# Nine weight buffers, each with its own order of words: interleaving the two parts, the two k tiles and the columns

## The chip, the cores and the metric

One core of one Trainium2 chip runs the whole kernel in one launch. The metric is the device time of that launch in microseconds (us), the median over the runs. Durations of single instructions below are in nanoseconds (ns) where they say so.

## The reference

A two-layer encoder trunk on 256 tokens of width 2048, in float32. Layer 0 mixes with neighbourhood attention and sliding-window attention, layer 1 with differential attention; both layers then have cross-attention to 256 memory tokens and an MLP of width 8192 with a squared ReLU. Around every part stands an RMS norm. Cut to what matters here:

```python
def squared_relu_mlp(h, w_up, w_down):          # w_up (2048, 8192), w_down (8192, 2048)
    u = jax.nn.relu(h @ w_up)
    return (u * u) @ w_down

for layer in range(2):
    proj = rms_norm(h, mix_pre_g[layer]) @ w_in   # (2048, 4608) even, (2048, 6144) odd
    y = attention(proj) @ w_out                   # (2048, 2048)
    h = h + rms_norm(y, mix_post_g[layer])
    c = memory_cross_attention(rms_norm(h, mem_pre_g[layer]), mem_n, wq, wk, wv, wo)
    h = h + rms_norm(c, mem_post_g[layer])
    f = squared_relu_mlp(rms_norm(h, mlp_pre_g[layer]), w_up[layer], w_down[layer])
    h = h + rms_norm(f, mlp_post_g[layer])
```

## The kernel before

Every product is done in three matmuls. Both operands are split into a high part, rounded to the type fp32r, and a low part, the rest; high times high, high times low and low times high are added in PSUM (mm3, line 255; the list of pairs is PAIRS). An fp32r matmul takes a stationary operand of 128 x 128, which a weight load (LDWEIGHTS, shown as engine PEld) brings in, and streams a moving operand of up to 512 columns past it.

The weights come from memory once. Weights.load (line 177) makes one weight tile: a DMA on the queue of SP brings 256 rows by 512 columns as two k tiles of 128 rows into a buffer "raw" (three of them), ScalarE writes the high part (line 188, or 193 with the norm's gain) and VectorE the low part, raw minus high (line 189, or 194). The tile is called w and has on each partition 2 parts x 2 k tiles x 512 columns of four bytes, 8 KiB. Tiles rotate through NW = 9 buffers of the pool wp, the nine "homes"; a few (11) go to tiles of other names that are free at the time (tags v, qT, kT, lt). A home is filled again when its last matmul is done; matmuls ask for tiles AHEAD = 4 tiles before they need them.

There are three uses of a weight tile:

- in_block / in_step (line 263): projections. x, transposed and split, is the stationary operand, the weights are the moving operand: w[:, b, kk, :], 512 columns. A tile serves 2 token tiles x 2 k tiles x 3 = 12 matmuls. In the profile this is `mm<-w,xT` of line 257.
- out_block (line 289): output projections and the MLP's down product. Again the weights move, 12 matmuls a tile: `mm<-w,lt` of line 257.
- up (line 686, groups 1 to 15 of each layer's 16): the MLP's up product. Here the weights are stationary: for each 128 columns of one k tile, the high part is loaded and both parts of x stream past it as 512 columns (line 718), then the low part, and the high part of x streams past as 256 columns (line 719). A tile serves 8 such pairs. Group 0 of each layer goes through in_block.

The order of TensorE's instructions is written out by hand (a manual schedule with a clock of its own, the class Line); the other engines follow by semaphores. A pool "shift" of X_SHIFT = 24 words stands between the long-lived tiles (h, y, xT) and wp, so that all homes begin 96 bytes after where they would begin.

Of the kernel before, what the change touches and what calls it, by code (L numbers as in the profile page):

```python
# [12 lines left out]
F32R = mybir.dt.float32r  # L13
# [17 lines left out]
NPB = 2  # L31
X_SHIFT = 24
NG = 16
D_TR, D_EV, D_ROPE = 8, 3, 8
SW_GAP, SW_T, SW_M = 4, 8, 7
NA_GAP, NA_T, NA_M = 5, 14, 9
# [35 lines left out]
def trunk(  # L72
# [8 lines left out]
    keep = ctx.enter_context(tc.tile_pool(name="keep", bufs=1))  # L81
    shift = ctx.enter_context(tc.tile_pool(name="shift", bufs=1))
    shift.tile([P, X_SHIFT], F32, name="shift")
    wp = ctx.enter_context(tc.tile_pool(name="wp", bufs=NW))
    rawp = ctx.enter_context(tc.tile_pool(name="rawp", bufs=3))
    gp = ctx.enter_context(tc.tile_pool(name="gp", bufs=1))
    sb = ctx.enter_context(tc.tile_pool(name="sb", bufs=1))
# [67 lines left out]
    class Weights:  # L155
        def __init__(self):
            self.specs, self.tiles, self.n, self.wait, self.open = [], {}, 0, [], set()
            self.goal, self.live = -1, 0

        def plan_in(self, src, n0, g, spare=(), gate=None):  # L160

# [7 lines left out]
        def plan_out(self, src, k0):  # L169
# [4 lines left out]
                    self.specs.append((src, k0 + 2 * kp, n * 512, None, None, None))  # L174
            return a

        def load(self, j):
            src, k0, n0, tag, _, g = self.specs[j]
            raw = rawp.tile([P, 2, 512], F32, tag="raw", name="raw")
            nc.sync.dma_start(  # L180
                raw, src[k0 * P : (k0 + 2) * P, n0 : n0 + 512].rearrange("(k p) n -> p k n", p=P)
            )
            if tag is None:
                w = wp.tile([P, 2, 2, 512], F32R, tag="w", name="w")
            else:
                w = sb.tile([P, 2, 2, 512], F32R, tag=tag, bufs=1, name="w")
            if g is None:
                A.copy(w[:, 0], raw)  # L188
                V.tensor_tensor(w[:, 1], raw, w[:, 0].bitcast(F32), ALU.subtract)  # L189
            else:  # L190
                for kk in range(2):
                    gk = gains[:, g * KT + k0 + kk : g * KT + k0 + kk + 1]
                    A.activation(w[:, 0, kk], raw[:, kk], AF.Copy, scale=gk)  # L193
                    V.scalar_tensor_tensor(  # L194
                        w[:, 1, kk], raw[:, kk], gk, w[:, 0, kk].bitcast(F32), ALU.mult, ALU.subtract
                    )
            self.tiles[j] = w
# [57 lines left out]
    def mm3(pt, lhs, rhs, first, last):  # L255
        for i, (a, b) in enumerate(PAIRS):
            PE.matmul(pt, lhs(a), rhs(b), start=first and i == 0, stop=last and i == 2)  # L257

    def xT_lhs(kt, t):
        return lambda a: xT[:, kt, a, t, :]  # L260

    def in_step(pt, u, kp, t):
        w = W.get(u + kp)
        line.until(lambda: I.has_x(t, kp // 2, W.specs[u + kp][5] >= G_MN))
        for kk in range(2):
            kt = 2 * kp + kk
            mm3(pt, xT_lhs(kt, t), lambda b: w[:, b, kk, :], kt == 0, kt == KT - 1)
            if kk == 1 and t == NT - 1:
                W.done(u + kp)
            line.tick()  # L270
# [19 lines left out]
    def out_block(u, lt, first, done=None, stagger=False):  # L290
        def chunk(t, n):
            pt = mm_ps()
            for kt in range(4):
                w = W.get(u + 2 * n + kt // 2)
                mm3(
                    pt, lambda a: lt[:, a, kt, t * P : (t + 1) * P], lambda b: w[:, b, kt % 2, :],
                    kt == 0, kt == 3,
                )
                if kt % 2 == 1 and t == NT - 1:
                    W.done(u + 2 * n + kt // 2)  # L300
                line.tick()
            ysl = y[:, t, n * 512 : (n + 1) * 512]
            if done is not None:
                if first:
                    done(t, n, pt)
                else:
                    V.tensor_tensor(ysl, pt, ysl, ALU.add)  # L307
                    done(t, n, ysl)
            elif first:
                A.copy(ysl, pt)  # L310
            else:
                V.tensor_tensor(ysl, pt, ysl, ALU.add)  # L312

        order = [(t, n) for t in range(NT) for n in range(4)]
        for t, n in order if stagger else sorted(order, key=lambda x: x[1]):
            chunk(t, n)
# [337 lines left out]
    def mem_and_mlp(l, R, kT, nxt):  # L654
        qT = qT_tile()

        def between(t):
            for n in range(4):
                mem_x(t, n)

        in_block(U["mq", l], evac_T(qT, R, q=True, ev=D_EVM), lag=L_MQ, between=between)
        v = v_tile()
        hd = Heads(qT, kT, lambda i: i, v, lambda i: i, tags=("pT", "pT", "qT", "kT"), lag=(ME_GAP, ME_T, ME_M)).start(M_AT, mix=False)
        in_block(U["mv", l], evac_V(v, RSM), lag=L_MV)
        for i in range(4):
            line.until(lambda: hd.pT[i] is not None)
            hd.mix(i)
        lv = Leave(gain(mem_post_g[l : l + 1]), G_MLP + l)
        hd.finish()
        W.free(("up", l))  # L670
        out_block(U["mo", l], hd.lt, True, lv, stagger=True)
        R = lv.next

        def split_u(ut, j, pts):

            s = sb.tile([P, 512], F32, tag="p", bufs=NPB, name="s")
            for i, pt in enumerate(pts):
                e = sb.tile([P, S], F32, tag="ue", bufs=2, name="ue")
                A.copy(e, pt[:, S:])  # L679
                V.tensor_tensor(s[:, i * S : (i + 1) * S], pt[:, :S], e, ALU.add)  # L680
            A.activation(s, s, AF.Relu)
            A.activation(s, s, AF.Square)
            d = [ut[:, a, j : j + 2, :].rearrange("p k c -> p (k c)") for a in range(2)]
            split_to(d[0], d[1], s)

        def up(g):
            ut = lt_tile(("lt", "qT")[g % 2])
            if g == 0:
                left = [0, 1]

                def ev(t, pt):
                    q = sb.tile([P, 512], F32, tag="q", bufs=2, name="u")
                    A.activation(q, pt, AF.Relu)

                    def turn():
                        tp = tr_ps()
                        for i in range(4):
                            PE.transpose(tp[:, i * P : (i + 1) * P], q[:, i * P : (i + 1) * P], ident)
                        s = sb.tile([P, 512], F32, tag="p", bufs=NPB, name="s")
                        A.activation(s, tp, AF.Square)  # L700
                        sv = s.rearrange("p (k c) -> p k c", c=P)
                        split_to(ut[:, 0, :, t * P : (t + 1) * P], ut[:, 1, :, t * P : (t + 1) * P], sv)

                    line.later(D_EVU, turn)

                in_block(U["up", l, 0], ev, lag=L_UP)
                return ut
            pts = [at_ps() for _ in range(3)] + [mm_ps()]
            for kp in range(8):
                w = W.get(U["up", l, g] + kp)  # L710
                for t in range(NT):
                    line.until(lambda: I.has_x(t, kp // 2, False))
                for nt in range(4):
                    for kk in range(2):
                        kt = 2 * kp + kk
                        wn = [w[:, a, kk, nt * P : (nt + 1) * P] for a in range(2)]
                        both = xT[:, kt].rearrange("p a t c -> p (a t c)")
                        PE.matmul(pts[nt], wn[0], both, start=kt == 0, stop=False)  # L718
                        PE.matmul(pts[nt][:, :S], wn[1], both[:, :S], start=False, stop=kt == KT - 1)  # L719
                    if nt == 3:  # L720
                        W.done(U["up", l, g] + kp)
                    line.tick()
            for b in range(2):
                split_u(ut, 2 * b, pts[2 * b : 2 * b + 2])
            return ut

        uts = {0: up(0)}
        lv = None
        for g in range(NG):
            if g + 1 < NG:  # L730
                uts[g + 1] = up(g + 1)
            last = g == NG - 1
            if last and l == 0:
                W.free("odd")
            if last:
                eps = []
                for r in R:
                    q = sm.tile([P, 1], F32, tag="r2", name="r2")
                    V.tensor_tensor(q, r, r, ALU.mult)
                    V.reciprocal(q, q)  # L740
                    V.tensor_scalar(q, q, q, NEPS, ALU.mult, ALU.mult)
                    eps.append(q)
                lv = Leave(gain(mlp_post_g[l : l + 1]), nxt, eps)
            out_block(U["dn", l, g], uts.pop(g), g == 0, lv, stagger=last)
        return lv.next
# [233 lines left out]
```

## Time and profile before

| | us |
|---|---|
| median of 2 runs | 2386.59 |
| lowest, highest | 2384.79, 2388.38 |
| the profiled execution, time | 2386.64 |
| the profiled execution, span from the first to the last instruction | 2384.8 |
| mean granted TensorE clock in the span | 0.997 of full |

The profile shows one execution, whose time is 0.05 us from the median. PE is TensorE's matmuls, PEld its weight loads, DVE is VectorE, ACT is ScalarE, L257 is line 257. Matmuls overlap: the duration of one is from its start to the end of its last column through the array, so what a stream of them costs is read from start to start and not from the mean duration.

### The profile page before, as it was taken

How to read it: one execution, taken by the hardware profiler on the slowest of the kernel's cores; microseconds unless marked ns; L12 is line 12 of the kernel's file. 1: busy time of each engine (PE TensorE's matmuls, PEld its weight loads, DVE VectorE, ACT ScalarE, POOL GpSimd, SP SyncE). 2: the span in 40 equal slices, each digit the busy share in tenths (PEclk: the TensorE clock that was granted, in tenths of full speed). 3: DMA queues.
4: the chain of work that ended last, by engine and by line, in shares of the span. 5: the costliest groups of instructions: out<-in, count | busy, mean ns of one | idle time of the engine just before them, and what ended most of it. 6: DMA issues, size and time to landing. Idle time of an engine off the chain costs nothing.

```text
span 2384.8 us, 32033 instructions
## 1 busy us (share of the span) xinstructions
PE 2359.4 (99%) x11687; PEld 1985.5 (83%) x11687; DVE 1610.2 (68%) x2545; ACT 1374.4 (58%) x2280; POOL 28.0 (1%) x46
## 2 busy tenths in 40 slices
PE   8999999999999999999999999999999999999998
PEld 7788888888888888888888888887888888888887
DVE  5766678856656656656876667787666666666666
ACT  6756567755545545545666555676655555555543
POOL 0000000000000000000000000000000000000000
PEclk9999999999999999999999999999999999999999
DMA  7657655565665665665565555655665565665663
GB/s 240 217 181 236 187 192 194 183 203 179 194 194 181 194 195 182 195 193 186 184 194 170 172 189 169 200 186 177 198 194 187 186 196 184 191 196 180 194 194 114
DMA packets 238278, 451.88 MB, mean 189 GB/s; under 512 B 21288, under 2 KB 22184, under 8 KB 237352
## 3 DMA queue, kind: packets, MB, share of 16 engines
q1 hardware_dynamic: 237832, 449.32, 59.3%
q8 instruction: 91, 1.49, 0.3%
q14 instruction: 67, 0.55, 0.1%
q10 hardware_dynamic: 288, 0.52, 0.1%
HBM read 445.59 MB, written 5.15 MB: 189 GB/s over the span
## 4 chain that ended last, share of the span: by engine, by line
PE 91%; DMA 3%; DVE 3%; ACT 1%; issue 1%; POOL 0%; SPq 0%; DVEq 0%; POOLq 0%; ACTq 0%
PE mm L257 59%; PE at L718 14%; PE at L719 7%; PE mm L718 5%; PE mm L719 2%; PE at L257 2%; DVE w L194 1%; DMA mt<-memT 1%; DMA raw<-in_even_w_in 1%; DMA raw<-in_mem_wv 1%; PE tr L435 1%; PE tr L348 1%; DMA h<-in_x 0%; PE at L505 0%; DVE xT L341 0%
## 5 line engine op out<-in xcount | busy, mean ns | idle before, releaser
L257 PE MATMUL mm<-w,lt 128*128 128x512 f32 x4032 | 927.7, 390 | 0.0
L257 PEld LDWEIGHTS mm<-w,lt 128*128 128x128 f32 x4032 | 752.6, 188 | 155.7
L194 DVE SCALAR_TENSOR_TENSOR w<-raw,gains,w 128x512 fp32r<-128x512 f32 x944 | 677.7, 747 | 267.9 <-ACT w L193 266.0
L193 ACT ACTIVATE w<-raw,gains 128x512 fp32r<-128x512 f32 x944 | 635.7, 717 | 358.5 <-PE mm L257 267.2
L257 PE MATMUL mm<-w,xT 128*128 128x512 f32 x2784 | 676.1, 396 | 2.1 <-ACT q L427 1.9
L189 DVE TENSOR_TENSOR w<-raw,w 128x1024 fp32r<-128x1024 f32 x336 | 411.2, 1224 | 385.4 <-ACT w L188 384.8
L188 ACT CAST w<-raw 128x1024 fp32r<-128x1024 f32 x336 | 353.4, 1052 | 447.2 <-PE mm L719 348.1
L257 PEld LDWEIGHTS mm<-w,xT 128*128 128x128 f32 x2784 | 515.0, 189 | 104.6 <-ACT q L427 2.3
L718 PE MATMUL at<-xT,w 128*128 128x512 f32 x1440 | 519.6, 399 | 0.0
L719 PE MATMUL at<-xT,w 128*128 128x256 f32 x1440 | 404.4, 281 | 0.0
L718 PEld LDWEIGHTS at<-xT,w 128*128 128x128 f32 x1440 | 270.6, 188 | 66.8
L719 PEld LDWEIGHTS at<-xT,w 128*128 128x128 f32 x1440 | 272.0, 189 | 1.2
L312 DVE TENSOR_TENSOR y<-mm,y 128x512 f32<-128x512 f32 x256 | 175.5, 686 | 16.8 <-PE mm L257 16.7
L718 PE MATMUL mm<-xT,w 128*128 128x512 f32 x480 | 180.4, 399 | 0.0
L719 PE MATMUL mm<-xT,w 128*128 128x256 f32 x480 | 134.7, 281 | 0.0
L718 PEld LDWEIGHTS mm<-xT,w 128*128 128x128 f32 x480 | 90.2, 188 | 22.7
L719 PEld LDWEIGHTS mm<-xT,w 128*128 128x128 f32 x480 | 90.7, 189 | 0.0
L679 ACT COPY ue<-at 128x256 f32<-128x256 f32 x90 | 33.2, 369 | 31.3 <-PE mm L718 28.2
L399 DVE TENSOR_TENSOR lt<-s,lt 128x512 fp32r<-128x512 f32 x64 | 44.1, 688 | 3.6 <-ACT lt L398 3.6
L257 PEld LDWEIGHTS at<-kT,qT 128*128 128x128 f32 x240 | 35.4, 196 | 8.9 <-ACT qT L398 3.5
L325 POOL TENSOR_TENSOR rr<-rb,mhalf 128x1 f32<-128x1 f32 x26 | 19.0, 730 | 1989.0 <-DVE rb L383 1696.1
L321 ACT ACTIVATE junk<-y 128x512 bf16<-128x512 f32 x32 | 20.1, 629 | 38.5 <-DVE y L307 38.2
(113 smaller groups left out, 1082.6 us busy)
## 6 DMA issues: line engine op xcount, KB each, us to landing
raw<-in_mlp_w_up SPq DMA_DIRECT2D x256, 512.0 KB, 3.8
raw<-in_mlp_w_down SPq DMA_DIRECT2D x256, 512.0 KB, 4.3
raw<-in_odd_w_in SPq DMA_DIRECT2D x96, 512.0 KB, 4.2
raw<-in_even_w_in SPq DMA_DIRECT2D x72, 512.0 KB, 4.5
raw<-in_even_w_out SPq DMA_DIRECT2D x32, 512.0 KB, 4.4
raw<-in_odd_w_out SPq DMA_DIRECT2D x32, 512.0 KB, 3.7
mt<-memT SPq DMA_DIRECT2D x32, 256.0 KB, 4.0
raw<-in_mem_wk SPq DMA_DIRECT2D x16, 512.0 KB, 4.4
```

What stands on the lines that cost most here:

```text
L188: A.copy(w[:, 0], raw)
L189: V.tensor_tensor(w[:, 1], raw, w[:, 0].bitcast(F32), ALU.subtract)
L193: A.activation(w[:, 0, kk], raw[:, kk], AF.Copy, scale=gk)
L194: V.scalar_tensor_tensor(w[:, 1, kk], raw[:, kk], gk, w[:, 0, kk].bitcast(F32), ALU.mult, ALU.subtract)
L257: PE.matmul(pt, lhs(a), rhs(b), start=first and i == 0, stop=last and i == 2)
L312: V.tensor_tensor(ysl, pt, ysl, ALU.add)
L348: PE.transpose(pt[:, i * P : (i + 1) * P], h[:, t, k * P : (k + 1) * P], ident)
L399: V.tensor_tensor(lo, src, hi.bitcast(F32), ALU.subtract)
L435: PE.transpose(tp[:, i * P : (i + 1) * P], u[:, i * P : (i + 1) * P], ident)
L679: A.copy(e, pt[:, S:])
L718: PE.matmul(pts[nt], wn[0], both, start=kt == 0, stop=False)
L719: PE.matmul(pts[nt][:, :S], wn[1], both[:, :S], start=False, stop=kt == KT - 1)
```

## The change

The nine homes become nine tags of one buffer each, taken in turn as before. Each home has its own order of the words of a tile on a partition, from HOMES: a = the two parts, k = the two k tiles, m = blocks of columns, q = the columns of a block. With "a k m q" and 512 the 512 columns of one part and one k tile stand together, as before (homes 0 and 1). With "k m a q" and 1 the two parts of each column stand side by side, so that the columns of one part lie 2 words apart (home 2); "a m k q" and 1 does so with the two k tiles (home 3); "m k a q" and 1 with both, so that the columns of one part and k tile lie 4 words apart (home 4). "m k a q" with 4, 8 and 32 leaves runs of 4, 8 and 32 columns together and puts the runs 16, 32 and 128 words apart (homes 5, 6, 7); "k m a q" with 16 has runs of 16 columns, 32 words apart (home 8).

Tiles of the MLP's up weights (gain groups G_MLP and G_MLP + 1) take their home's order only in the homes with 1 (2, 3 and 4), the plain order in the others. ScalarE and VectorE write each tile in its home's order, and the matmuls read it so, by the new function cols. Instructions, their number, their shapes in elements, the DMAs and the order of the work stay.

```diff
 NG = 16
+HOMES = (
+    ("a k m q", 512), ("a k m q", 512), ("k m a q", 1), ("a m k q", 1), ("m k a q", 1),
+    ("m k a q", 4), ("m k a q", 8), ("m k a q", 32), ("k m a q", 16),
+)
-    wp = ctx.enter_context(tc.tile_pool(name="wp", bufs=NW))
+    wp = ctx.enter_context(tc.tile_pool(name="wp", bufs=1))
+        def home(self, stationary):
+            i = self.turn = (self.turn + 1) % NW
+            c, (order, q) = "abcdefghi"[i], HOMES[i]
+            if stationary and q > 1:
+                order, q = HOMES[0]
+            t = wp.tile([P, 2 * 2 * 512], F32R, tag=f"w{c}", name=f"w{c}")
+            return t.rearrange(f"p ({order}) -> p a k m q", a=2, k=2, q=q)
         def load(self, j):
             if tag is None:
-                w = wp.tile([P, 2, 2, 512], F32R, tag="w", name="w")
+                w = self.home(g in (G_MLP, G_MLP + 1))
             else:
-                w = sb.tile([P, 2, 2, 512], F32R, tag=tag, bufs=1, name="w")
+                w = sb.tile([P, 2, 2, 1, 512], F32R, tag=tag, bufs=1, name="w")
+            raw = raw.rearrange("p k (m q) -> p k m q", q=w.shape[4])
+    def cols(w, a, kk, lo, n):
+        q = w.shape[4]
+        if q >= n:
+            return w[:, a, kk, lo // q, lo % q : lo % q + n]
+        if q == 1:
+            return w[:, a, kk, lo : lo + n, 0]
+        return w[:, a, kk, lo // q : (lo + n) // q, :]
-            mm3(pt, xT_lhs(kt, t), lambda b: w[:, b, kk, :], kt == 0, kt == KT - 1)
+            mm3(pt, xT_lhs(kt, t), lambda b: cols(w, b, kk, 0, 512), kt == 0, kt == KT - 1)
-                    pt, lambda a: lt[:, a, kt, t * P : (t + 1) * P], lambda b: w[:, b, kt % 2, :],
+                    pt, lambda a: lt[:, a, kt, t * P : (t + 1) * P], lambda b: cols(w, b, kt % 2, 0, 512),
-                        wn = [w[:, a, kk, nt * P : (nt + 1) * P] for a in range(2)]
+                        wn = [cols(w, a, kk, nt * P, P) for a in range(2)]
```

## Rows read from the trace of the kernel before

**Rows 1.** The page's part 1: busy time, share of the span, instructions

```profile
PE 2359.4 (99%) x11687; PEld 1985.5 (83%) x11687; DVE 1610.2 (68%) x2545; ACT 1374.4 (58%) x2280; POOL 28.0 (1%) x46
```

**Rows 2.** The page's part 4: the chain that ended last, by engine and by line

```profile
PE 91%; DMA 3%; DVE 3%; ACT 1%; issue 1%; POOL 0%; SPq 0%; DVEq 0%; POOLq 0%; ACTq 0%
PE mm L257 59%; PE at L718 14%; PE at L719 7%; PE mm L718 5%; PE mm L719 2%; PE at L257 2%; DVE w L194 1%; DMA mt<-memT 1%; DMA raw<-in_even_w_in 1%; DMA raw<-in_mem_wv 1%; PE tr L435 1%; PE tr L348 1%; DMA h<-in_x 0%; PE at L505 0%; DVE xT L341 0%
```

**Rows 3.** Instructions on the weights: count, duration min/median/max, first and last start

```profile
L257 PE MATMUL mm<-w,lt x4032: 387/389/481, 94.1 to 2376.0; 128*128 128x512 f32 x192
L257 PEld LDWEIGHTS mm<-w,xT x2784: 186/188/338, 9.2 to 1687.7; 128*128 128x128 f32 x199
L257 PE MATMUL mm<-w,xT x2784: 387/389/776, 9.3 to 1688.0; 128*128 128x512 f32 x199
...
L718 PE MATMUL at<-xT,w x1440: 389/398/477, 475.3 to 2331.6; 128*128 128x512 f32 x180
L719 PEld LDWEIGHTS at<-xT,w x1440: 187/189/192, 475.4 to 2331.6; 128*128 128x128 f32 x180
...
L193 ACT ACTIVATE w<-raw,gains x944: 702/716/766, 7.8 to 2309.5; 128x512 fp32r<-128x512 f32 x189
...
L718 PE MATMUL mm<-xT,w x480: 395/398/403, 477.5 to 2332.3; 128*128 128x512 f32 x160
...
L188 ACT CAST w<-raw x336: 1029/1052/1070, 73.4 to 2353.3; 128x1024 fp32r<-128x1024 f32 x168
L189 DVE TENSOR_TENSOR w<-raw,w x336: 1215/1226/1229, 74.5 to 2354.4; 128x1024 fp32r<-128x1024 f32 x168
```

**Rows 4.** Timeline of PE, 100 to 115 us: start, time, what, count

```profile
99.78 15.58 PE L257 MATMUL mm<-w,lt 128*128 128x512 f32 x68
```

**Rows 5.** Chain in order of time, two of the 28 equal pieces: start, time, what

```profile
498.55 21.78 PE mm L257 x96
...
2288.43 21.79 PE mm L257 x96
```

**Rows 6.** Timelines of PE from 63.9 and from 66.2 us

```profile
63.57 3.16 PE L257 MATMUL mm<-w,xT 128*128 128x512 f32 x7
...
65.70 1.03 PE L257 MATMUL mm<-w,xT 128*128 128x512 f32 x2
```

**Rows 7.** Windows: stretch, length, PE, PEld, DVE, ACT, POOL busy, PEclk, DMA, GB/s

```profile
63.20:66.50 3.30, 3.30 (x9) 2.60 (x8) 2.83 (x9) 2.96 (x5) 0.00 (x0) 0.50 0.97 353
...
100.00:115.00 15.00, 15.00 (x68) 12.41 (x67) 8.50 (x12) 10.54 (x18) 0.00 (x0) 1.00 0.53 168
```

**Rows 8.** Timeline of PE in an up group, from 700.16 us

```profile
700.18 0.40 PE L718 MATMUL mm<-xT,w 128*128 128x512 f32 x1
700.41 0.28 PE L719 MATMUL mm<-xT,w 128*128 128x256 f32 x1
700.53 0.40 PE L718 MATMUL at<-xT,w 128*128 128x512 f32 x1
...
701.13 0.28 PE L719 MATMUL at<-xT,w 128*128 128x256 f32 x1
701.24 0.40 PE L718 MATMUL at<-xT,w 128*128 128x512 f32 x1
```

**Rows 9.** Groups by line: two operations of 512 elements on ACT and DVE

```profile
L399 DVE TENSOR_TENSOR lt<-s,lt 128x512 fp32r<-128x512 f32 x64 | 44.1, 688 | 3.6 <-ACT lt L398 3.6
L398 ACT CAST lt<-s 128x512 fp32r<-128x512 f32 x64 | 39.0, 610 | 0.2
```

**Rows 10.** Windows of one down and up group of the MLP, columns as in rows 7

```profile
853.64:898.03 44.39, 44.39 (x226) 37.62 (x225) 28.54 (x39) 23.31 (x35) 0.00 (x0) 1.00 0.60 190
```

More of the change, by code (lines that the diff above doesn't have):

```diff
@@ L157, in __init__ @@
             self.specs, self.tiles, self.n, self.wait, self.open = [], {}, 0, [], set()
-            self.goal, self.live = -1, 0
+            self.goal, self.live, self.turn = -1, 0, -1
         def plan_in(self, src, n0, g, spare=(), gate=None):
```

## The prediction

> **What bounds the kernel now.** I read the page's busy shares first. PE is busy for 2359.4 us of 2384.8, DVE for 68%, ACT for 58% [rows 1]. The chain that ended last says the same more sharply: 91% of it is PE, nearly all matmuls that read weight tiles (59% line 257 with weights moving, 28% lines 718 and 719 with weights stationary), and only 1% is DVE's writing of w [rows 2]. So time changes here if the stream of matmuls runs at another rate, and hardly otherwise.
>
> The rate of that stream is read from the timeline, from start to start. Between 100 and 115 us 68 matmuls of 512 columns take 15.58 us, the last one 0.39: (15.58 - 0.39) / 67 = 226.7 ns each [rows 3, 4]. In the chain's list 96 of them take 21.78 us, 226.9 ns each, and 28 pieces of the whole run agree within 0.01 us [rows 5]. Two things are to be seen. First, no address makes a difference: these pieces pass through all nine homes, both parts and both k tiles, and they are equal. Second, 226.7 ns is more than 512 columns at 2.4 GHz, 213.3 ns, although the granted clock there is 1.00 [rows 7]: 13.3 ns, one cycle in 17, is lost. In the short stretch at 63 to 66.5 us, where the granted clock is 0.50 (1.2 GHz), five matmuls start in 65.70 - 63.57 = 2.13 us, 426 ns each [rows 6, 7]: 512 / 1.2 = 426.7, nothing lost. So at the full clock the array asks for more words than it gets. It gets 512 / 226.7 = 2.26 words per ns and partition, at the lower clock 1.2 without loss. I take this as a limit in the supply of the moving operand. The trace proves a loss, not where it arises.
>
> In the up groups three pairs of a 512 and a 256 column matmul take 701.24 - 700.18 = 1.06 us, 353 ns a pair [rows 8], against 340 at the rate above.
>
> **The change, part by part.** No instruction, DMA or wait is added, and the homes are taken in the same turn. What changes is how far apart the words lie that one instruction reads or writes. I count the tiles first. 944 writes by line 193 make 472 tiles (two each), and 336 by line 188 make 336: 808, of which 11 go to other names, 797 to homes. The 1440 + 480 instructions of line 718 are 1920 pairs, 8 to a tile: 240 tiles with stationary weights [rows 3]. The other 557, at 12 matmuls, are 6684 moving matmuls, 743 a home on average. Following the turn through the plan of loads gives 756 for home 4, 1500 for homes 2 and 3 together, 732 each for homes 5, 6 and 8, 744 for home 7, and 26 stationary tiles (208 pairs) in home 4.
>
> (1) *Moving reads in home 4*, every fourth word. No row shows a word stride, so I bound it. From below: nothing (226.7 ns stays). Next row: 426.7 ns, one column per cycle of 1.2 GHz [rows 6]. From above: supply at half its present rate, 453.4 ns, or at a quarter, 906.8, if all that is fetched between the words is lost. The supply is already the limit with words side by side, and this order asks it for four times the span of addresses; if anything pays for spacing, it is this home first. I take 426.7, the one slower rate that the trace shows: 756 x (426.7 - 226.7) = +151 us; with 453.4 it is +171.
>
> (2) *Moving reads in homes 2 and 3*, every second word, 1500 matmuls. Bounds: a gain of 13.3 ns each (the loss goes; -20 us) and 200 ns each (+300). I take nothing: half of each stretch fetched is still used, and the span asked for only doubles. The upper end is a rival below.
>
> (3) *Moving reads of runs of 4 to 32 words* (homes 5 to 8, 2940 matmuls). Bounds: -13.3 ns each (-39 us), and +40 ns in home 5 with +13.3 in home 6, from a loss per piece touched (rival below; +39 us). I take nothing.
>
> (4) *Stationary reads in homes 2 to 4.* A weight load lasts 189 ns [rows 3], but the next matmul starts 113 to 120 ns after the 256-column one [rows 8], so a load beside that matmul has no cover. Beside the 512-column one (some 236 ns) there is more than 100 ns. If 128 weights in home 4 come at half the rate, that is 128 / 2.4 = 53 ns more, on the path once a pair: 208 x 53 = +11 us, which I take. Bounds: 0, and +149 ns (338 at most, the load at the lower clock [rows 3]), with some 30 more beside the long one: 179 x 208 = +37. For homes 2 and 3 I take nothing.
>
> (5) *Writes by ACT and DVE.* ACT takes 1052 ns for 1024 elements and 610 for 512, so 0.86 ns an element; DVE 1226 and 688, 1.05 [rows 3, 9]. If spacing doubles that, one tile costs ACT 884 and DVE 1076 ns more; in homes 2 to 4 that is 3.2 us of DVE per nine tiles. Nine tiles are PE's work for 9 x 12 x 226.7 ns = 24.5 us, and DVE idles about 36% of it in an MLP group (28.54 busy of 44.39), ACT 47% [rows 10]: 8.7 and 11.6 us. With four tiles asked for ahead this is hidden; I cost it at nothing. If the cover goes, it is where the chain already runs through w on DVE, 1% or 24 us [rows 2]; if those writes double in a third of the tiles, +8 us.
>
> Sum: 2386.64 (the profiled time; the median, 2386.59, is the same within 0.1) + 151 + 11 = 2549 us.
>
> [...]
>
> **The rivals.** *No effect*: the lost 13.3 ns belong to the array and not to the supply, and spaced words are fetched as fast. For it: 226.7 is so even that it looks like a fixed rhythm [rows 4, 5]; against: the loss vanishes at the lower clock, where less is asked for. 2387 us. Chance 0.28.
>
> *Two words at a time*: the supply brings pairs of neighbouring words, so homes 2, 3 and 4 all fall to 426.7. For it: 2.26 words per ns is just under two per cycle of 1.2 GHz; against: nothing shows the width. 2256 x 200 = 451, and 53 ns on some 630 pairs = 33: 2871 us. Chance 0.13.
>
> *A loss per piece*: the 32 cycles lost in 512 columns are one per 16 words, 64 bytes; orders that touch more such pieces lose more, 0.42 ns each. Homes 4 and 5 touch 128 instead of 32: +40 ns x 1488 = 59.5; homes 2, 3 and 6 touch 64: +13.3 x 2232 = 29.7. 2387 + 89 = 2476 us. Chance 0.10.
>
> *Faster*: the loss comes from neighbouring words hitting the same place twice in a row, and orders that spread them lose nothing. Place: moving reads of homes 2 to 8, 756 + 1500 + 2940 = 5196 matmuls x 13.3 = -69 us, 2317 us. It passes 2% (47.7 us) only if at least 3590 of these matmuls, five homes of seven, are freed and home 4 doesn't pay. For it: the loss is real; against: it is the same in all nine homes and at every piece [rows 5], and nothing shows what would cure it. Chance 0.07.
>
> **How the numbers follow.** The forecast, home 4 alone, has 0.42. Its own range is 2510 to 2615: from a price of some 150 ns, to 453 ns with the upper weight load (171 + 37) and 13 ns each in homes 2 and 3 (20). A measurement of this kernel can tell about 2% from no change. Faster: 0.07. Within 2%: 0.28, the no-effect case. Slower: 0.42 + 0.13 + 0.10 = 0.65. The range of 8 in 10 takes in no effect, the loss per piece and the forecast, from 2375 to 2640, and leaves out the two ends (0.20).
>
> **What would show it.** After the change the matmuls `mm<-w,lt` should fall into two kinds: 12 in a row at about 427 ns from start to start, once in nine tiles, and all others at 227. Their sum should make up the difference, with PE still 99% busy and the chain still PE. If two or three homes in nine show it, the two-word rival is right; if home 5 shows about 267 ns, the loss per piece; if PE's idle time grows, releasers being w on ACT or DVE, then (5) was costed wrongly. If every start lies at 227 the forecast is wrong, and at 213 the faster rival holds. In the up groups one tile in nine should show pairs of about 406 ns. DVE and ACT may show longer writes in homes 2 to 4 without effect on the span.

## The result: 23.5% slower

The changed kernel takes 2945.74 us (median of 2 runs, 2944.82 to 2946.67) against 2386.59: a ratio of 1.2352, interval 1.2327 to 1.2377. That is 559 us more. The forecast was 2549, with 2375 to 2640 as the range, and lies far below. The profiled execution took 2946.67 us, its span is 2944.6 and the granted clock 0.998. The page of the changed kernel answers to [rows 1, 2] so:

```profile
PE 2921.2 (99%) x11687; PEld 2067.7 (70%) x11687; DVE 1695.6 (58%) x2545; ACT 1472.4 (50%) x2280; POOL 28.9 (1%) x46
...
PE 96%; DVE 1%; DMA 1%; ACT 1%; issue 0%; SPq 0%; DVEq 0%; POOLq 0%; ACTq 0%
```

The counts are the same. PE is still busy for 99% of a longer span and is now 96% of the chain instead of 91%. Its idle time is 2944.6 - 2921.2 = 23.4 us, where it was 25.4 [rows 1]: the whole loss lies in the stream of matmuls, and no new wait has come in. The nine homes now have names of their own, wa to wi for homes 0 to 8, so the timeline of PE can be read home by home. Here is one stretch of a down product (start, time, what, count):

```profile
2291.06 2.88 PE L272 MATMUL mm<-wc,lt 128*128 128x512 f32 x6
2293.75 2.89 PE L272 MATMUL mm<-wd,lt 128*128 128x512 f32 x6
2296.46 2.89 PE L272 MATMUL mm<-wc,lt 128*128 128x512 f32 x6
2299.17 2.89 PE L272 MATMUL mm<-wd,lt 128*128 128x512 f32 x6
2301.87 2.95 PE L272 MATMUL mm<-we,lt 128*128 128x512 f32 x6
2304.64 1.59 PE L272 MATMUL mm<-wf,lt 128*128 128x512 f32 x6
2306.07 2.92 PE L272 MATMUL mm<-we,lt 128*128 128x512 f32 x6
...
2310.22 1.58 PE L272 MATMUL mm<-wg,lt 128*128 128x512 f32 x6
2311.64 1.59 PE L272 MATMUL mm<-wh,lt 128*128 128x512 f32 x6
2313.06 1.59 PE L272 MATMUL mm<-wg,lt 128*128 128x512 f32 x6
...
2317.36 1.55 PE L272 MATMUL mm<-wa,lt 128*128 128x512 f32 x6
2318.75 1.58 PE L272 MATMUL mm<-wi,lt 128*128 128x512 f32 x6
```

From start to start, divided by six: wc (home 2) 2.69 / 6 = 448 ns, wd (home 3) 2.71 / 6 = 452, we (home 4) 2.77 / 6 = 462, wf, wg and wh (homes 5 to 7) 1.43 / 6 and 1.42 / 6 = 237 to 238, wa (home 0) 1.39 / 6 = 232. So three homes pay, and with nearly the same price; the others read here are 5 to 11 ns above the 226.7 of before.

The stationary side and the writes are seen in the rows of instructions by tile (duration min/median/max in ns), first home 2, then home 4:

```profile
L741 PEld LDWEIGHTS at<-xT,wc x156: 193/196/198, 627.6 to 2861.8; 128*128 128x128 f32 x156
L742 PEld LDWEIGHTS at<-xT,wc x156: 193/197/201, 627.7 to 2861.9; 128*128 128x128 f32 x156
...
L208 ACT ACTIVATE wc<-raw,gains x102: 732/755/774, 12.8 to 2835.8; 128x512 fp32r<-128x512 f32 x102
L209 DVE SCALAR_TENSOR_TENSOR wc<-raw,gains,wc x102: 742/748/755, 13.8 to 2838.4; 128x512 fp32r<-128x512 f32 x102
...
L741 PEld LDWEIGHTS at<-xT,we x156: 308/310/315, 663.9 to 2868.0; 128*128 128x128 f32 x156
L742 PEld LDWEIGHTS at<-xT,we x156: 312/334/338, 664.1 to 2868.2; 128*128 128x128 f32 x156
L208 ACT ACTIVATE we<-raw,gains x104: 1161/1261/1339, 19.5 to 2845.8; 128x512 fp32r<-128x512 f32 x104
L209 DVE SCALAR_TENSOR_TENSOR we<-raw,gains,we x104: 1134/1204/1276, 20.9 to 2847.8; 128x512 fp32r<-128x512 f32 x104
```

With 2 words from column to column a weight load lasts 196 ns instead of 189 and a write of ACT 755 instead of 716 [rows 3]; with 4 words the loads go to 310 and 334, ACT's write to 1261, VectorE's to 1204 (748 with 2 words). In an up tile of home 4 the eight pairs then take 3.77 us, 471 ns each, instead of 353 [rows 8]:

```profile
2330.01 0.52 PE L741 MATMUL at<-xT,we 128*128 128x512 f32 x1
2330.37 0.28 PE L742 MATMUL at<-xT,we 128*128 128x256 f32 x1
2330.49 0.51 PE L741 MATMUL at<-xT,we 128*128 128x512 f32 x1
...
2333.78 0.40 PE L741 MATMUL at<-xT,wf 128*128 128x512 f32 x1
```

The gap that grows is the one after the 512-column matmul (360 ns between the first two rows, 230 in [rows 8]), not the one after the 256-column matmul (120).

### The profile page after: what moved, and what is told of

Same layout as the page of the kernel before. It is cut to its first block, busy times and chain, and to the rows that moved or that the text cites. A ratio compares the mean times of both kernels' runs of the same rounds, so it can differ in the third digit from the quotient of the medians.

```text
span 2944.6 us, 32033 instructions
## 1 busy us (share of the span) xinstructions
PE 2921.2 (99%) x11687; PEld 2067.7 (70%) x11687; DVE 1695.6 (58%) x2545; ACT 1472.4 (50%) x2280; POOL 28.9 (1%) x46
## 4 chain that ended last, share of the span: by engine, by line
PE 96%; DVE 1%; DMA 1%; ACT 1%; issue 0%; SPq 0%; DVEq 0%; POOLq 0%; ACTq 0%
PE mm L272 69%; PE at L741 12%; PE at L742 6%; PE mm L741 4%; PE mm L742 2%; PE at L272 2%; PE tr L371 1%; PE tr L458 1%; DMA h<-in_x 0%; PE at L528 0%; DMA mt<-memT 0%; ACT we L203 0%; DMA bias<-scr 0%; DVE we L204 0%; DMA raw<-in_mem_wo 0%
## 5 line engine op out<-in xcount | busy, mean ns | idle before, releaser
L272 PE MATMUL mm<-wc,lt 128*128 128x512 f32 x456 | 219.3, 630 | 0.0
L272 PE MATMUL mm<-we,lt 128*128 128x512 f32 x444 | 217.8, 641 | 0.0
L272 PE MATMUL mm<-wd,lt 128*128 128x512 f32 x444 | 214.8, 633 | 0.0
L209 DVE SCALAR_TENSOR_TENSOR we<-raw,gains,we 128x512 fp32r<-128x512 f32 x104 | 122.7, 1202 | 112.8 <-ACT we L208 112.7
L208 ACT ACTIVATE we<-raw,gains 128x512 fp32r<-128x512 f32 x104 | 122.4, 1260 | 129.4 <-PE mm L272 122.1
L272 PE MATMUL mm<-we,xT 128*128 128x512 f32 x312 | 152.6, 648 | 0.0
L272 PE MATMUL mm<-wc,xT 128*128 128x512 f32 x300 | 143.6, 634 | 0.0
L272 PE MATMUL mm<-wd,xT 128*128 128x512 f32 x300 | 143.4, 636 | 0.0
L272 PE MATMUL mm<-wh,lt 128*128 128x512 f32 x468 | 124.4, 401 | 0.0
L272 PE MATMUL mm<-wa,lt 128*128 128x512 f32 x468 | 120.7, 393 | 0.0
```

The lines of the kernel that those rows point to most:

```text
L209: V.scalar_tensor_tensor(w[:, 1, kk], raw[:, kk], gk, w[:, 0, kk].bitcast(F32), ALU.mult, ALU.subtract)
```

## The experiments

All kernels below are the changed one with other tables, or the kernel before with one number changed. For the former, tiles with moving weights take their order from HOMES, up tiles from a second table STAT (plain unless said), and a tile with moving weights can begin OFFS words later in its home, which is PAD words larger (both 0 unless said). From the kernels with pairs on, the up tiles of group 0, whose weights move, go by HOMES too (n0 > 0 in the last line). Where no number of runs stands beside a time, it is that of one run; the runs of the kernel before lay between 2382 and 2391 us.

```diff
-            c, (order, q) = "abcdefghi"[i], HOMES[i]
-            if stationary and q > 1:
-                order, q = HOMES[0]
-            t = wp.tile([P, 2 * 2 * 512], F32R, tag=f"w{c}", name=f"w{c}")
+            c, (order, q) = "abcdefghi"[i], (STAT if stationary else HOMES)[i]
+            t = wp.tile([P, 2 * 2 * 512 + PAD], F32R, tag=f"w{c}", name=f"w{c}")
+            o = 0 if stationary else OFFS[i]
+            t = t[:, o : o + 2 * 2 * 512]
...
-                w = self.home(g in (G_MLP, G_MLP + 1))
+                w = self.home(g in (G_MLP, G_MLP + 1) and n0 > 0)
```

After the result the forecast's step (2), by which every second word costs nothing, was already hurt by homes 2 and 3 (448 and 452 ns). Two theories of mine stood against each other: words come in neighbouring pairs; or any step but 1 in the innermost dimension halves the rate. That some larger unit has to be used whole was thought of only after the runs with pairs.

**All homes plain, through the new code.**

```diff
-HOMES = (("a k m q", 512), ("a k m q", 512), ("k m a q", 1), ...)
+HOMES = (("a k m q", 512),) * 9
```

> All nine homes in the plain order, but through the new code (nine tags of one buffer, function cols). If the loss lies in the orders alone, every moving matmul starts 227 ns after the last and the time is that of before, 2387 us within 5. If the nine tags or another place of the homes cost something (homes 0 and 1, which are plain, ran at 233 and 231 ns on average in the changed kernel), it is 2387 + 6684 x 5 ns = 2420 us.

Measured: 2385.37 us in 10 runs, ratio 0.9997 (0.9988 to 1.0007). The nine tags and the function cols cost nothing that these runs can tell; the orders are the whole of it.

**Homes 2, 3 and 4 plain, the runs stay.**

```diff
-    ("k m a q", 1), ("a m k q", 1), ("m k a q", 1),
+    ("a k m q", 512), ("a k m q", 512), ("a k m q", 512),
```

> The changed kernel with homes 2, 3 and 4 plain; homes 5 to 8 keep their runs of 4, 8, 32 and 16 columns. If the spaced single words carry nearly all of the loss, 2387 + 2940 x 12 ns = 2422 us, with no matmul near 450 ns. If part of what the changed kernel lost in homes 2 to 4 is a wait for slower writes, nothing of it is left either, and the time is the same; if runs pay more when no home is slower, over 2450.

Measured: 2408.23 us, ratio 1.0099 (1.0082 to 1.0116). The three homes with single words carry 2945.74 - 2408.23 = 537.5 us of the 559, the runs of 4 to 32 columns 21.6 us, or 7 ns for each of their 2940 matmuls, where the expectation had 12 ns and 2422 us.

**Pairs of columns in homes 2, 3 and 4, on an even word and on an odd one.** Two kernels; the second only moves the tiles by a word.

```diff
-    ("k m a q", 1), ("a m k q", 1), ("m k a q", 1),
+    ("m k a q", 2), ("m k a q", 2), ("m k a q", 2),
-    ("m k a q", 4), ("m k a q", 8), ("m k a q", 32), ("k m a q", 16),
+    ("a k m q", 512), ("a k m q", 512), ("a k m q", 512), ("a k m q", 512),
```

```diff
+PAD = 8
+OFFS = (0, 0, 1, 1, 1, 0, 0, 0, 0)
```

> Homes 2, 3 and 4 keep pairs of columns together (order m k a q with blocks of 2 columns, 8 words from pair to pair), all else plain. Pair theory (the moving stream is read two neighbouring words at a time, and a read that gives one useful word takes as long): 227 to 240 ns in these homes, 2387 to 2417 us. Step theory (any step but 1 in the innermost dimension halves the rate): the same. [...] Loss per 64-byte piece touched: 128 pieces, +40 ns, 2387 + 2256 x 40 ns = 2477 us. Loss per run: 256 runs, well over that.

> As the pairs before, but in homes 2, 3 and 4 every tile with moving weights begins one word later, so that each pair of columns straddles the border of two 8-byte pairs of addresses. Pair theory with fixed pairs of addresses: every column needs a read of its own, 453 ns, 2387 + 2256 x 226 ns = 2897 us. Step theory, or pairs that may begin at any word: as without the shift, 2387 to 2417 us.

Measured: 2900.93 and 2920.3 us. The first overturned every theory under which pairs are cheap, and a price per piece would have given 2477: pairs that stand together on an even word are as slow as single words. The second is 19 us slower still, and as its three homes cost no more than in the first, this lies in the plain homes, whose places had moved too and whose matmuls went from 227 ns to 231 and 234. The timeline of the first, one stretch of a down product, then two rows of the second:

```profile
2379.05 2.95 PE L291 MATMUL mm<-wc,lt 128*128 128x512 f32 x6
2381.82 2.95 PE L291 MATMUL mm<-wd,lt 128*128 128x512 f32 x6
2384.59 2.95 PE L291 MATMUL mm<-we,lt 128*128 128x512 f32 x6
2387.35 1.56 PE L291 MATMUL mm<-wf,lt 128*128 128x512 f32 x6
```

```profile
2339.65 2.94 PE L291 MATMUL mm<-wd,lt 128*128 128x512 f32 x6
2342.41 2.95 PE L291 MATMUL mm<-we,lt 128*128 128x512 f32 x6
```

2.77 / 6 and 2.76 / 6 = 460 to 462 ns in each of the three homes, and 2.76 / 6 = 460 in the second kernel. The innermost step is 1 here, so a step other than 1 isn't what costs, and neither do neighbouring pairs help, whether they begin on an even word or on an odd one. Runs of 4 cost 238 in home 5 of the changed kernel. What remained, as a reading of these times (460 ns for pairs, 238 for runs of 4), was a unit of four words, 16 bytes (called a line here), that has to be used whole: the line theory of the next run. A high price for each of the 256 runs would have fitted this run alone, but the 128 runs of home 5 cost only 11 ns together.

**Where a run begins.** One kernel, a different case in each home; PAD is 16.

```diff
+HOMES = (("a k m q", 512), ("a k m q", 512), ("m k a q", 4), ("m k a q", 4), ("m k a q", 8),
+    ("m k a q", 4), ("k m a q", 2), ("k m a q", 256), ("m k a q", 128))
+OFFS = (1, 2, 1, 2, 2, 4, 0, 0, 0)
```

> Each home tries another case with moving weights (up weights plain). Homes 0 and 1: plain order, begun 1 and 2 words (4 and 8 bytes) later. Homes 2 and 3: runs of 4 columns, begun 1 and 2 words later. Home 4: runs of 8, 2 words later. Home 5: runs of 4, 4 words later. Home 6: runs of 2, 4 words from run to run. Homes 7 and 8: runs of 256 and 128. Line theory (full rate only where four neighbouring columns are one aligned 16-byte line, else one column per cycle of 1.2 GHz): homes 0 and 1 about 227 ns by lines read ahead, 2 and 3 453 to 461, 4 between, about 344, 5 240, 6 453 to 461, 7 and 8 227 to 240; time 2387 + 174 + 171 + 87 + 9 + 165 = 2990 us. Run theory (the innermost run must count four columns or more, wherever it begins): homes 0 to 5 227 to 240, only 6 at 453 to 461; 2387 + 36 + 165 = 2590 us. If each four columns are taken as a group and must lie in one line even in a plain row, homes 0 and 1 too go to 453: over 3300 us.

Measured: 2980.13 us, where the line theory said 2990, the run theory 2590 and the group theory over 3300. PE's timeline in a down product:

```profile
2326.35 2.85 PE L291 MATMUL mm<-wd,lt 128*128 128x512 f32 x6
2329.01 2.87 PE L291 MATMUL mm<-wc,lt 128*128 128x512 f32 x6
2331.68 2.86 PE L291 MATMUL mm<-wd,lt 128*128 128x512 f32 x6
2334.35 2.34 PE L291 MATMUL mm<-we,lt 128*128 128x512 f32 x6
2336.51 1.58 PE L291 MATMUL mm<-wf,lt 128*128 128x512 f32 x6
2337.93 2.31 PE L291 MATMUL mm<-we,lt 128*128 128x512 f32 x6
...
2341.47 2.90 PE L291 MATMUL mm<-wg,lt 128*128 128x512 f32 x6
2344.19 1.57 PE L291 MATMUL mm<-wh,lt 128*128 128x512 f32 x6
2345.60 2.90 PE L291 MATMUL mm<-wg,lt 128*128 128x512 f32 x6
...
2351.14 1.58 PE L291 MATMUL mm<-wa,lt 128*128 128x512 f32 x6
2352.55 1.57 PE L291 MATMUL mm<-wi,lt 128*128 128x512 f32 x6
```

Runs of 4 begun one or two words late (wc, wd): 2.67 / 6 = 445 and 2.66 / 6 = 443 ns. Begun one word late (wc), three words of a run share a line, and even three don't help: 445 ns. The same runs begun four words late, on a 16-byte border again if a home begins on one (wf): 1.42 / 6 = 237. Runs of 8 begun two words late, of which half the columns make a whole line (we): 2.16 / 6 = 360, between the two. Pairs of which each shares its line with a pair of the other part (wg): 2.72 / 6 = 453. A plain row begun one word late (wa): 1.41 / 6 = 235. So what counts is the place of the words against borders 16 bytes apart, counted from the start of a home, for each line by itself: 237 ns with all columns in whole lines, 360 with half, 443 to 453 with none. The three cases with runs of 4 are the same instructions but for their addresses.

**The stationary side alone, by 4 words and by 2.**

```diff
+HOMES = (("a k m q", 512),) * 9
+STAT = (("m k a q", 1),) * 9
```

```diff
+HOMES = (("a k m q", 512),) * 9
+STAT = (("k m a q", 1),) * 9
```

> Only the stationary up weights are spaced, in all nine homes by 4 words (order m k a q with 1); all moving weights plain. If the weight load alone makes the 116 ns that a pair of lines 741 and 742 lost in home 4 of the changed kernel: 1920 x 116 ns = +223, 2610 us, with loads of 310 to 336 ns. If part of it came from the neighbours (other homes, slower writes), less; if the spaced writes of ACT and DVE, twice as long, now bind in the MLP, more, with waits on w.

> Only the stationary up weights are spaced, in all nine homes by 2 words (order k m a q with 1). [...] If a weight load suffers from a step of 2 as the moving stream does, 53 ns a pair or more: 1920 x 53 ns = +102, 2489 us.

Measured: 2611.46 and 2387.55 us; the first as expected within 2 us, and the second as the kernel before beside it (2387.34), where loads that suffer as the moving stream does would have given 2489. The rows by tile, home 4 (we) in the kernel with 4 words, then in the one with 2:

```profile
L760 PEld LDWEIGHTS at<-xT,we x156: 308/310/311, 533.3 to 2548.4; 128*128 128x128 f32 x156
...
L761 PEld LDWEIGHTS at<-xT,we x156: 310/334/338, 533.5 to 2548.6; 128*128 128x128 f32 x156
```

```profile
L760 PEld LDWEIGHTS at<-xT,we x156: 193/196/198, 524.5 to 2326.6; 128*128 128x128 f32 x156
...
L761 PEld LDWEIGHTS at<-xT,we x156: 193/197/201, 524.6 to 2326.7; 128*128 128x128 f32 x156
```

With 2 words from column to column a weight load takes 196 and 197 ns, where it took 189 [rows 3], and the time stays; with 4 words it takes 310 and 334 ns, 121 to 145 more. The first kernel also writes all 240 up tiles spaced by 4 words, and its time is met by the pairs alone (2387 + 1920 x 116 ns = 2610 us): the slower writes cost it nothing that shows.

**All moving weights by 2 words.**

```diff
+HOMES = (("k m a q", 1),) * 9
```

> All moving weights in all nine homes with 2 words from column to column (order k m a q with 1), up weights plain. If the price holds per matmul whatever the neighbours, 2387 + 6684 x 223 ns = 3877 us. In a stretch at the low clock: if spacing costs a fixed supply of one column per cycle of 1.2 GHz, a 512-column matmul takes 427 to 453 ns there too; if spacing halves the rate at any clock, 853 ns.

Measured: 3863.12 us, 14 below what a fixed price gives for nine homes instead of three: within 1% the price is one of the matmul, not of its neighbours. The part on the low clock stayed open, as this execution had no such stretch with spaced weights.

**Spaced weights at the low clock.**

```diff
+HOMES = (("k m a q", 1), ("m k a q", 1)) * 4 + (("k m a q", 1),)
...
+    idle = sm.tile([P, 1], F32, tag="idle", name="idle")
+    for _ in range(160):
+        sumsq(idle, h[:, 0, 0:512])
     hd = sw(1, qT)
```

> All moving weights spaced, by 2 words in homes 0, 2, 4, 6 and 8 (k m a q, 1) and by 4 in the others (m k a q, 1), and 160 idle sums of squares (0.63 us each, 100 us) put into ACT's queue ahead of layer 0's second sliding-window block, so that PE runs out of weights there and starts again at the low clock on spaced weights. The extra sums are added work, not part of the reference. One column per cycle of 1.2 GHz as a fixed supply: at the low clock a 512-column matmul of either spacing starts 427 to 461 ns after the last, no slower than at the full clock. Halved at any clock: 853 ns there. The time says little: about 2387 + 3732 x 223 + 2952 x 232 ns = 3904 us, and up to 100 more.

Measured: 3945.01 us. The timeline of PE, three starts by 2 words at about 100 us, six at 2809 us by 4 words, and twelve by 2 words at the full clock; then the windows with the granted clock (the column after the busy times):

```profile
100.63 2.90 PE L291 MATMUL mm<-wa,xT 128*128 128x512 f32 x6
...
101.99 1.54 PE L291 MATMUL mm<-wa,xT 128*128 128x512 f32 x3
...
2809.68 2.94 PE L291 MATMUL mm<-wf,lt 128*128 128x512 f32 x6
2812.45 2.89 PE L291 MATMUL mm<-wg,lt 128*128 128x512 f32 x6
...
110.66 5.61 PE L291 MATMUL mm<-wc,xT 128*128 128x512 f32 x12
116.09 4.33 PE L291 MATMUL mm<-wd,xT 128*128 128x512 f32 x9
```

```profile
100.00:103.00 3.00, 3.00 (x8) 1.99 (x8) 2.08 (x3) 3.00 (x4) 0.00 (x0) 0.50 0.51 139
110.00:113.00 3.00, 3.00 (x8) 1.31 (x7) 2.58 (x3) 2.97 (x5) 0.00 (x0) 1.00 0.81 203
2810.20:2813.40 3.20, 3.20 (x9) 2.15 (x8) 3.01 (x5) 2.01 (x4) 0.00 (x0) 0.50 0.58 166
```

At the granted clock 0.50 matmuls on spaced words start every 1.36 / 3 = 453 ns (by 2) and 2.77 / 6 = 462 (by 4; the first of these six starts just before that stretch), at 1.00 every 5.43 / 12 = 452.5. The granted clock makes no difference to them here. Plain rows take 426 at the low clock [rows 6] and 226.7 at the full one. An estimate from these times: a supply of about one read in 453 / 512 = 0.885 ns at both clocks, from which a plain row at the full clock gets two columns in the same time, 226.7 / 256 = 0.886. No row shows such a read.

**Runs of 32 in all homes; the homes 32 bytes earlier.** Two kernels about the few ns of the other homes; the second is the kernel before.

```diff
+HOMES = (("m k a q", 32),) * 9
```

```diff
-X_SHIFT = 24
+X_SHIFT = 16
```

> All moving weights in runs of 32 columns, 128 words from run to run (m k a q, 32), in all nine homes; up weights plain. If runs of whole lines cost a matmul the same few ns wherever they stand (9 ns in homes 5 to 8 of the run without spaced words): 2387 + 6684 x 9 ns = 2447 us. If that cost came from neighbours in other orders, 2387 to 2400.

> The kernel before with X_SHIFT 16 in place of 24, so that all homes begin 32 bytes earlier against x and the other long-lived tiles; every order plain. In the run with pairs begun one word late the plain homes, moved by multiples of 32 bytes, went from 227 to 231 to 234 ns. If the place of a home against the stationary operand makes such few ns: 2387 + 2784 x 5 ns to 6684 x 5 ns, 2400 to 2420 us. If not, 2387.

Measured: 2447.66 us and 2383.72 (before 2389.27 beside them). Runs of 32 cost (2447.66 - 2389.27) / 6684 = 9 ns a matmul in all nine homes. It isn't a price per run, since in the changed kernel runs of 4 (128 in a matmul) and of 32 (16) pay alike, 238 and 237 ns. In the second kernel the total stayed within 0.3%, so the 2400 to 2420 us of the expectation did not come; its parts did move, as the next kernel takes up.

**Two places for two uses.** In the kernel with X_SHIFT 16 the trace shows pairs of lines 718 and 719 at 347 ns instead of 353, and moving weights against x at 233 instead of 228.5. The two cancel: 1920 x 6 ns less and 2784 x 4.5 ns more, 12 us each. I tried to take the better of both:

```diff
+HOMES = (("a k m q", 512),) * 9
+PAD = 32
-            o = 0 if stationary else OFFS[i]
+            o = 24 if stationary else OFFS[i]
```

> All orders plain; each home 32 words (128 bytes) larger, tiles with moving weights at its start and up tiles 24 words later, which puts these where the run with X_SHIFT 16 has them (8 words earlier, by steps of 32). There the pairs of lines 741/742 took 347 ns instead of 353 and the moving weights against x 233 instead of 228.5. If the place against x decides each by itself: pairs at 347, moving weights at 227 to 228.5, 2387 - 1920 x 6 ns = 2375 us, 0.5% below before. If the larger homes move other tiles to worse places, 2387 or more.

Measured: 2394.98 us in 5 runs, ratio 1.0035 (1.0022 to 1.0049). The pairs came out as hoped, 8 in 2.78 us:

```profile
1100.36 0.39 PE L760 MATMUL at<-xT,we 128*128 128x512 f32 x1
...
1103.14 0.40 PE L760 MATMUL at<-xT,wf 128*128 128x512 f32 x1
```

But moving weights against lt rose from 227 to between 230 and 234 ns (means by home), by turns from home to home; no run shows why. The kernel came out 0.35% slower than before, and none of these kernels is faster than it by more than its own runs differ.

## Why the prediction was wrong, step by step

The reading of what bounds the kernel was right: the time follows the rate of matmuls on weights, no wait came in, and the price of a home sits in its own matmuls. The assumption that the 13.3 ns lost per matmul mark a limit in the supply of the moving operand, which the prediction could not prove, is supported by the low-clock run: words spaced by 2 cost 453 ns at both clocks, and 226.7 is half of that. The prediction's 1.2 GHz is a rate of columns, 512 in 426 ns at the granted clock 0.50 [rows 6, 7]. The 2.4 GHz is an estimate, twice that rate at 1.00, and so are the 213.3 ns and what is counted in cycles: no row shows a clock in GHz, or plain rows faster than one in 226.7 ns. "No address makes a difference" was read too widely: it holds for the pieces against lt that were read, but 32 bytes moved the matmuls against x from 228.5 to 233 ns.

Step (1), home 4: the price came, its size was off. Taken was 426.7 ns, measured 462: 756 x (462 - 226.7) = 178 us in place of 151. The row chosen, a plain row at the low clock, goes with the clock (426 ns at 0.50, 226.7 at 1.00), and spaced words don't (453 and 452.5), so it could not show their rate. The end not taken, 453.4, was nearer.

Step (2), homes 2 and 3, is the step that failed: "half of each stretch fetched is still used". That was my estimate, and no run shows it for the moving stream. Measured 448 and 452 in place of 226.7: 1500 x 225 (with 452) = 338 us where I took nothing, and more than the 200 ns of the upper bound. This one step is six tenths of the result. Its upper bound of +300 us stood in the working, but entered the forecast only as a rival outside the range.

Step (3), the runs: 21.6 us where I took 0 with bounds of -39 and +39. Step (4): 471 - 353 = 118 ns a pair in home 4 instead of 53, 208 x 118 = 25 us in place of 11, and on the other matmul of the pair than I thought; nothing in homes 2 and 3, as taken (2387.55 us with all up weights spaced by 2). Step (5): the writes of home 4 became 1.6 to 1.8 times as long (512 columns: ACT 1261 ns for 716, VectorE 1204 for 747) and about 1.7 and 2.0 times (1024 columns: VectorE 2070 for 1226, ACT 2075 for 1052), and stayed hidden, as said: PE idles 23.4 us, before 25.4.

The terms add up: 178 + 338 + 22 + 25 = 563 us, of 559 measured.

The rival "two words at a time" came nearest (2871 us, chance 0.13), for the three homes that it named, but its mechanism fell too: pairs on even words take 460 to 462 ns. Its price, again 426.7, left it 75 us short. The range left it out. "No effect" (0.28) fell with the time, "loss per piece" would have made home 5 267 ns and fell with 238, and "faster" fell with no home below 226.7.

The operands did not pay alike. A weight load took 196 ns with 2 words from column to column and 310 to 334 with 4 (189 before), a write of ACT 755 and 1261 ns (716 before). TensorE's moving stream of four-byte words at the full clock took 448 to 462 ns with two words of a line, 462 with one, and only with all four 227 to 242 (the last in home 8). Step (2) made no difference between the operands.

What stays open: why a line used in half (448 to 462 ns) gives hardly more than a line used for one word (462), and what makes the 5 to 12 ns of the other homes, in which a division into runs (9 ns) and the places of the two operands (228.5 to 233 ns by 32 bytes) both have a part, but not the number of runs (238 ns with 128, 237 with 16).

## What to carry to other kernels

Keep a moving operand of four-byte words in whole, aligned groups of four columns. At the full clock, runs of only 1 or 2 columns cost twice the time of the matmul here (448 to 462 ns for 226.7), a run of 4 that begins one or two words late nearly so (443 to 445), and an aligned run of 4 237 to 238. Stationary operands spaced by 2 words loaded in 196 ns, where plain ones took 189, and the time stayed (2387.55 us); ACT's writes spaced by 2 words took 5% longer (755 ns for 716 in home 2) without effect on the time. When a cost has no row, look whether one price holds for all operands of an instruction, and let the range hold the case in which it doesn't: here three homes against one made most of the difference between 2549 and 2946.

## What the runs showed of the hardware that was not expected

The rate of spaced words was the same at both granted clocks of TensorE: 453 ns for 512 columns at 0.50 and 452.5 at 1.00 by 2 words, 462 at both by 4. A step of 4 words is hardly dearer than one of 2 (462 and 452), so the price isn't in the span of addresses. And a matmul whose runs straddle lines pays by the line: 360 ns where half of the columns stand in whole lines, 443 to 445 where none do, though in one of these two cases three words of four share a line.
